# First pair's expert rows half gathered and half built, and one more weight buffer, in a two-layer mixture-of-experts encoder

## The chip, the cores and the metric

The kernel runs on one core of a Trainium2 chip. A core has TensorE (PE), which multiplies and transposes, VectorE (DVE), ScalarE (ACT), GpSimd (POOL) and SyncE (SP), which here issues nearly all weight transfers. Sixteen DMA engines bring data from device memory. The metric is the time of one execution on the device in microseconds (us).

## The reference

Two layers are computed on 512 tokens of width 1024. Each layer has a mixer (three kinds of attention) and then an expert-choice feed-forward part. Cut to what matters here, the second part is:

```python
def expert_choice_ffn(h, w_router, w_gate, w_up, w_down):
    affinity = jax.nn.softmax(h @ w_router, axis=-1)           # 512 tokens, 16 experts
    gate, idx = lax.top_k(jnp.swapaxes(affinity, 1, 2), 64)    # each expert takes 64 tokens
    xe = h[idx]                                                # rows of the chosen tokens
    a, u = xe @ w_gate[e], xe @ w_up[e]                        # 1024 -> 1408
    y = (jax.nn.silu(a) * u) @ w_down[e]                       # 1408 -> 1024
    return scatter_add(y * gate)                               # back to the tokens
```

`h` is the RMS-normalised `x`: each row is scaled by its own factor (`rstds`) and each feature by a gain (`gf`). All of it is in float32.

## The kernel before, in words

The 16 experts are taken as 8 pairs. An expert takes 64 tokens, so a pair fills 128 rows. Of each pair, `xe` holds the chosen rows feature-major, as 8 blocks `xe[:, k]` of 128 features by 128 rows.

**Weights.** For each pair the loop at L1206 loads 24 weight tiles of 1408 KB with `load` (L152): eight of `w_gate` (k = 0 to 7), eight of `w_up`, eight of `w_down`. In this text weight tile n of a layer is the n-th load, so that tiles 0 to 7 are the first pair's `w_gate`, 8 to 15 its `w_up`, 16 to 23 its `w_down`. The room of a tile comes from `extra` (L1088): `SEQ` (L35) gives the first 15 rooms in order (eleven rooms `x0` to `x10`, the three rooms `s0` to `s2` of another pool, and once the room `hx`), and after that 14 rooms (all but `hx`) come round in the same order. A load is issued from SP's queue in program order, and it waits there until the tile that last had the room has been used by TensorE. So load 15 waits for tile 0, load 16 for tile 1, and so on; from load 27 on it is always the tile 14 loads before. The first 15 loads are issued while the mixer and the router are still running.

**Rows of the first pair.** `places(0)` (L1116) makes a 0/1 matrix `at` scaled with `rstds`, in the room `xy`. `fill` (L1128) makes one block of `xe` as a product of `x` with `at` (4 products, 8 PE instructions), and VectorE multiplies by `gf` on the way out. `EARLY` (L57) says after which k which blocks are filled: block 0 ahead of tile 0, blocks 1 and 2 after it, and then one after each of the tiles 1 to 5.

**Rows of the other pairs.** `marks(p)` (L1140) compares the ranks with `iota` on VectorE (`oh`), multiplies on TensorE for each row's token number, scale and gate, and transposes `oh`; VectorE copies the results out. `fetch_rows(p)` (L1159) then lets GpSimd gather the 128 rows of 4 KB from `xrow_d` in device memory into `xy`, and ScalarE scales them (L1163). `turn_rows` (L1166) transposes four blocks (L1170), and VectorE multiplies them by `gf` (L1171). `marks(p + 1)` and the gather stand after k = 6 of pair p's `w_gate`; the transposes stand, in the program, after the pair's `w_up`. For pair 0 `marks(0)` is wanted only for the gates and the scatter, and stands after k = 2 of `w_up`.

**Order.** The framework orders each engine's instructions by a plan of its own. `keep_in_program_order` ties an instruction behind the one that was written ahead of it for the same engine. The weight products (L1215, L1252), the loads, the `fill` calls inside the loop and the comparison in `marks` are tied; the products and transposes in `marks` and the transposes of `turn_rows` are not, and may be taken earlier than they are written.

Of the kernel before, what the change touches and what calls it, by code (L numbers as in the profile page):

```python
# [22 lines left out]
P = 128  # L23
S = 512
# [7 lines left out]
CAP = 64  # L32
SLOT = 3072
RING = 3
SEQ = [0, 1, 4, 's0', 2, 3, 's2', 5, 6, 7, 9, 8, 'hx', 10, 's1']  # L35
PAD = 168
AFTER = [[2, 3, 5, 8], [1, 5, 7, 10], [2, 3, 6, 9]]
H_ON = 'vvvvavaa'
# [15 lines left out]
PLAN = [(0, 1), (1, 1), (2, 2), (3, 2), (4, 2), (0, 0), (1, 2), (5, 2)]  # L54
PART_ON = 'vvav'
START = [[6, 0, 2, 6, 4], [2, 0, 0, 4, 2]]
EARLY = [[(0, 1)], [(1, 1), (2, 1)], [(3, 1)], [(4, 1)], [(5, 1)], [(6, 1)], [(7, 1)], [], []]  # L57
END_ON = 'avavav'
MARK_AT = 6
VALUES_AT = 9  # L60
FIRST_MARKS = 2
SCATTER_AT = (2, 4)
HALVED = 8
EASE = 5
# [66 lines left out]
def body(ctx, tc, x_in, pos, w_in, w_uq, w_ukv, w_out, w_gate, w_up, w_down, gatt, gfin, params, consts, band, sel, out):  # L131
# [8 lines left out]
    def nm(s):  # L140
        uid[0] += 1
        return f"{s}_{uid[0]}"
# [711 lines left out]
    for l in range(L):  # L854
# [221 lines left out]
        with tc.tile_pool(name=f"fx{l}", bufs=1, reuse_waits="tile") as fx, tc.tile_pool(name=f"fw{l}", bufs=2, side="right", reuse_waits="tile") as fw:  # L1076
# [5 lines left out]
            def xslot(i):  # L1082
                return fx.tile([P, 2 * FF], F32, tag=f"x{i}", name=nm("xslot"))
# [3 lines left out]
            def extra():  # L1087

                n = hold["n"]
                hold["n"] += 1  # L1090
                again = [q for q in SEQ if q != "hx"]
                which = SEQ[n] if n < len(SEQ) else again[(n - len(SEQ)) % len(again)]
                if isinstance(which, int):
                    return first_x.pop(which) if which in first_x else xslot(which)
                return wide() if which == "hx" else slot(which)[:, : 2 * FF]
# [19 lines left out]

            def places(p):  # L1116

                at_ = fw.tile([P, D], F32, tag="xy", bufs=1, name=nm("at"))[:, :S].rearrange("p (t s) -> p t s", t=NT)
                for t in (0, 2):
                    chosen(at_, p, t, t + 2)  # L1120
                for t in range(NT):
                    if t < 2:
                        nc.scalar.activation(at_[:, t], at_[:, t], AF.Copy, scale=rstds[:, t : t + 1])
                    elif t % 2 == 0:
                        q = at_[:, t : t + 2]
                        nc.vector.tensor_tensor(q, q, rstds[:, t : t + 2].unsqueeze(2).to_broadcast([P, 2, P]), op=ALU.mult)
                return at_

            def fill(at_, xe, k0, n, pin=False):

                b = bank()
                for k in range(n):
                    c = (k0 + k) * P
                    for t in range(NT):
                        made = nc.tensor.matmul(b[:, k * P : (k + 1) * P], x[:, t, c : c + P], at_[:, t], start=(t == 0), stop=(t == NT - 1))
                        if pin:
                            tc.keep_in_program_order(made)
                nc.vector.tensor_tensor(xe[:, k0 : k0 + n, :], b[:, : n * P].rearrange("p (k s) -> p k s", k=n), gf[:, k0 : k0 + n].unsqueeze(2).to_broadcast([P, n, P]), op=ALU.mult)

            def marks(p):  # L1140

                oh = fw.tile([P, S], F32R, tag="oh", bufs=2, name=nm("oh"))
                o3 = oh.rearrange("p (t s) -> p t s", t=NT)
                tc.keep_in_program_order(chosen(o3, p, 0, NT))
                b, g = bank(), bank()
                for t in range(NT):
                    nc.tensor.matmul(g[:, 0:4], o3[:, t].bitcast(F32), info[:, t, p, :], start=(t == 0), stop=(t == NT - 1))
                for t in range(NT):
                    nc.tensor.transpose(b[:, t * P : (t + 1) * P], o3[:, t].bitcast(F32), ident)
                for i in range(2):  # L1150
                    nc.vector.tensor_copy(gates[64 * i : 64 * i + 64, p : p + 1], g[64 * i : 64 * i + 64, i : i + 1])
                if p > 0:
                    nc.vector.tensor_copy(token[:, p : p + 1], g[:, 2:3])
                    nc.vector.tensor_copy(scales[:, p : p + 1], g[:, 3:4])
                nc.vector.tensor_copy(oh, b)  # L1155
                return oh


            def fetch_rows(p):  # L1159

                v = fw.tile([P, D], F32, tag="xy", bufs=1, name=nm("rows"))
                nc.gpsimd.indirect_dma_start(v, None, xrow_d[l][:, :], bass.IndirectOffsetOnAxis(token[:, p : p + 1], 0))  # L1162
                nc.scalar.activation(v, v, AF.Copy, scale=scales[:, p : p + 1])  # L1163
                return v

            def turn_rows(v, xe, k0):  # L1166

                b = bank()
                for k in range(4):
                    nc.tensor.transpose(b[:, k * P : (k + 1) * P], v[:, (k0 + k) * P : (k0 + k + 1) * P], ident)  # L1170
                nc.vector.tensor_tensor(xe[:, k0 : k0 + 4, :], b.rearrange("p (k s) -> p k s", k=4), gf[:, k0 : k0 + 4].unsqueeze(2).to_broadcast([P, 4, P]), op=ALU.mult)  # L1171

            def gathered():
# [32 lines left out]
            for p in range(8):  # L1206
                acc = []
                for w in (w_gate, w_up):
                    bs = [bank() for _ in cuts]
                    acc.append(bs)  # L1210
                    for k in range(KD):
                        ws = load(w[l, p, k])
                        for b, (q0, qn) in zip(bs, cuts):
                            for i in range(2):
                                tc.keep_in_program_order(nc.tensor.matmul(b[64 * i : 64 * i + 64, : qn * NJ], xe[:, k, 64 * i : 64 * i + 64], ws[i][:, q0 * NJ : (q0 + qn) * NJ], start=(k == 0), stop=(k == KD - 1)))  # L1215
                        if w is w_gate and p == 0:
                            for f in EARLY[k + 1]:
                                fill(xg, xe, *f, pin=True)
                        if w is w_gate and k in SCATTER_AT and pending is not None:
                            scatter(*pending, 2 * SCATTER_AT.index(k))  # L1220
                        if w is w_up and k == FIRST_MARKS and p == 0:
                            ohs[0] = marks(0)
                        if w is w_gate and k == MARK_AT and p < 7:
                            ohs[p + 1] = marks(p + 1)
                            rows = fetch_rows(p + 1)
                hx = wide()
                hh, hT = hx[:, :FF].rearrange("p (j q) -> p j q", j=NJ), hx[:, FF:].rearrange("p (j s) -> p j s", j=NJ)
                for g, u, (q0, qn) in zip(acc[0], acc[1], cuts):
                    hv = hh[:, :, q0 : q0 + qn].rearrange("p j q -> p q j")
                    nc.scalar.activation(hv, g[:, : qn * NJ].rearrange("p (q j) -> p q j", j=NJ), AF.Silu)  # L1230
                    nc.vector.tensor_tensor(hv, u[:, : qn * NJ].rearrange("p (q j) -> p q j", j=NJ), hv, op=ALU.mult)  # L1231
                if p < 7:
                    nxt = gathered()
                    for k0 in (0, 4):
                        turn_rows(rows, nxt, k0)
                for j0, n in ((0, 4), (4, 4), (8, 3)):
                    b = bank()
                    for q in range(n):
                        nc.tensor.transpose(b[:, q * P : (q + 1) * P], hh[:, j0 + q, :], ident)
                    nc.vector.tensor_copy(hT[:, j0 : j0 + n, :], b[:, : n * P].rearrange("p (q s) -> p q s", q=n))  # L1240
                bs = [bank(), bank()]
                ahead = [(t, h) for t in range(NT - 1) for h in range(2)] if p == 7 else []
                whole = {}
                for lo in range(0, NJ * D, FF):
                    hi = lo + FF
                    ws = load(w_down[l, p, lo // FF])
                    e = lo
                    while e < hi:
                        j, h = e // D, e % D // 512
                        z = min(hi, (e // 512 + 1) * 512)  # L1250
                        for i in range(2):
                            tc.keep_in_program_order(nc.tensor.matmul(bs[h][64 * i : 64 * i + 64, e % 512 : e % 512 + z - e], hT[:, j, 64 * i : 64 * i + 64], ws[i][:, e - lo : z - lo], start=(j == 0), stop=(j == NJ - 1)))  # L1252
                        e = z
                    if ahead and lo > 0:
                        take_x(*ahead.pop(0))
                ys = results(p, bs)
                if p < 7:
                    pending = ohs.pop(p), ys
                    xe = nxt
# [133 lines left out]
```

## Time and profile before

| | |
|---|---|
| median of 3 runs | 1949.41 us (1947.63 to 1950.34) |
| the profiled execution: time, span | 1949.72 us, 1947.6 us |
| mean granted TensorE clock | 0.967 of full speed |
| busy share of the span: PE, DVE, ACT, POOL | 90%, 36%, 22%, 10% |
| moved by DMA | 646.71 MB, mean 332 GB/s |

The span runs from the first to the last instruction; the time is 2.1 us longer. The clock has two levels here: 1.00 in the rows is 2.4 GHz, 0.50 is 1.2 GHz. A row of a timeline gives start, duration, engine, line, operation, what it writes and reads, how many instructions were merged, and in brackets how long the engine had been idle and what ended it.

### The profile page before, as it was taken

The numbers are of one execution on the slowest core, as the hardware profiler recorded it, in microseconds if no ns is written. First come the engines' busy times: TensorE is split into PE (matmuls) and PEld (weight loads), VectorE is DVE, ScalarE is ACT, GpSimd is POOL, SyncE is SP. The second block draws the span as 40 slices with busy tenths as digits, with TensorE's granted clock in tenths as the row PEclk, the third lists the DMA queues.
The fourth block names the chain that finished last, engine by engine and source line by source line (L and its number), as shares of the span: only waits on it lengthen the run. The fifth ranks groups of instructions, "written<-read, shape, count | busy, mean of one in ns | idle before, by whom it ended". The sixth has DMA issues, their size and how long they took to land.

```text
span 1947.6 us, 22276 instructions
## 1 busy us (share of the span) xinstructions
PE 1747.3 (90%) x8894; PEld 914.8 (47%) x8894; DVE 709.2 (36%) x1483; ACT 426.2 (22%) x881; POOL 203.2 (10%) x230
## 2 busy tenths in 40 slices
PE   7999999898998988888899999998898998888887
PEld 6786665443333333333377856753333333333323
DVE  6877856121121111211168688551112112111112
ACT  4337951000100100000043489311100000001001
POOL 1314421000000000000013253100000000000000
PEclk8999998999999999999999999999999999999999
DMA  6765748899999999999938736689999999999996
GB/s 222 209 178 85 169 142 310 321 418 424 424 425 424 424 425 424 424 423 425 406 116 261 164 74 133 220 332 363 425 424 425 424 424 424 425 424 424 425 424 247
DMA packets 102471, 646.71 MB, mean 332 GB/s; under 512 B 11008, under 2 KB 28160, under 8 KB 53216
## 3 DMA queue, kind: packets, MB, share of 16 engines
q1 hardware_dynamic: 88336, 606.34, 77.7%
q0 software_dynamic: 11968, 35.02, 7.6%
q10 hardware_dynamic: 2064, 3.93, 0.6%
q8 instruction: 70, 1.15, 0.2%
q14 instruction: 33, 0.27, 0.0%
HBM read 616.55 MB, written 27.39 MB: 331 GB/s over the span
## 4 chain that ended last, share of the span: by engine, by line
DMA 43%; PE 38%; DVE 9%; issue 5%; ACT 3%; POOL 1%; SPq 0%; DVEq 0%; ACTq 0%; POOLq 0%
DMA xslot<-in_w_up_dram 13%; DMA xslot<-in_w_down_dram 10%; PE ps L1215 9%; DMA xslot<-in_w_gate_dram 8%; PE ps L732 7%; PE ps L1252 6%; DMA slot<-in_w_gate_dram 6%; PE ps L833 4%; DMA rows<-xrow_d,slots 4%; PE ps L741 2%; PE ps L650 2%; PE ps L633 1%; DVE sm L582 1%; DMA slot<-in_w_down_dram 1%; PE ps L493 1%
## 5 line engine op out<-in xcount | busy, mean ns | idle before, releaser
L1215 PE MATMUL ps<-xslot,xe 128*64 128x506 f32 (+1 forms) x2400 | 515.9, 575 | 29.1 <-DMA xslot<-in_w_up_dram 16.6
L1215 PEld LDWEIGHTS ps<-xslot,xe 128*64 128x64 f32 x2400 | 166.8, 140 | 351.7 <-issue 286.6
L1252 PE MATMUL ps<-xslot,hx 128*64 128x512 f32 (+3 forms) x1392 | 248.8, 506 | 22.5 <-DMA xslot<-in_w_down_dram 18.7
L1231 DVE TENSOR_TENSOR hx<-ps,hx 128x506 f32<-128x506 f32 (+1 forms) x48 | 43.0, 959 | 475.4 <-PE ps L1215 475.4
L1252 PEld LDWEIGHTS ps<-xslot,hx 128*64 128x64 f32 x1392 | 94.1, 137 | 165.0 <-issue 123.4
L1182 ACT ACTIVATE hx<-ps,gates 128x512 fp32r<-128x512 f32 x32 | 20.2, 683 | 675.9 <-PE ps L1252 675.9
L732 PE MATMUL ps<-xh,w 128*128 128x512 f32 (+1 forms) x448 | 147.6, 414 | 11.5 <-ACT xh L346 11.5
L1183 DVE SCALAR_TENSOR_TENSOR hx<-ps,gates,hx 128x512 fp32r<-128x512 f32 x32 | 22.6, 747 | 345.1 <-ACT hx L1182 345.1
L1215 PE MATMUL ps<-slot,xe 128*64 128x506 f32 (+1 forms) x648 | 140.0, 566 | 7.3 <-DMA slot<-in_w_gate_dram 5.7
L1193 DVE TENSOR_TENSOR x<-ps,x 128x512 f32<-128x512 f32 x112 | 69.6, 684 | 160.2 <-PE ps L1191 160.2
L589 ACT ACTIVATE P<-ps,sm 128x512 f32<-128x512 f32 x168 | 116.4, 702 | 32.1 <-DVE sm L582 30.9
L1162 POOL DMA_INDIRECT rows<-xrow_d,slots x14 | 13.8, 984 | 987.5 <-DVE oh L1155 914.6
L1163 ACT ACTIVATE rows<-rows,slots 128x1024 f32<-128x1024 f32 x14 | 16.1, 1147 | 444.9 <-DMA rows<-xrow_d,slots 444.9
L732 PEld LDWEIGHTS ps<-xh,w 128*128 128x128 f32 (+1 forms) x448 | 87.0, 195 | 35.7 <-ACT xh L346 12.5
L1215 PEld LDWEIGHTS ps<-slot,xe 128*64 128x64 f32 x648 | 45.1, 138 | 91.3 <-issue 74.7
L732 PE MATMUL ps<-xl,w 128*128 128x512 f32 (+1 forms) x224 | 85.7, 393 | 0.0
L1170 PE MATMUL ps<-ident,rows 128*128 128x128 f32 x112 | 27.0, 421 | 64.8 <-ACT rows L1163 64.8
L582 DVE TENSOR_REDUCE sm<-ps 128x1 f32<-128x512 f32 x120 | 78.9, 681 | 5.5 <-PE ps L567 4.9
L633 PE MATMUL ps<-ident,P 128*128 128x128 f32 x512 | 77.8, 275 | 1.2 <-ACT P L589 1.2
L1252 PE MATMUL ps<-slot,hx 128*64 128x512 f32 (+3 forms) x400 | 71.6, 497 | 6.3 <-DMA slot<-in_w_down_dram 4.8
L641 ACT COPY pt<-ps 128x512 f32<-128x512 f32 x118 | 68.8, 604 | 25.8 <-PE ps L633 25.5
L633 PEld LDWEIGHTS ps<-ident,P 128*128 128x128 f32 x512 | 62.5, 141 | 24.4 <-ACT P L589 7.0
(280 smaller groups left out, 2186.1 us busy)
## 6 DMA issues: line engine op xcount, KB each, us to landing
xslot<-in_w_gate_dram SPq DMA_DIRECT2D x100, 1408.0 KB, 26.4
xslot<-in_w_up_dram SPq DMA_DIRECT2D x100, 1408.0 KB, 27.0
xslot<-in_w_down_dram SPq DMA_DIRECT2D x100, 1408.0 KB, 27.0
slot<-in_w_gate_dram SPq DMA_DIRECT2D x28, 1408.0 KB, 27.0
slot<-in_w_down_dram SPq DMA_DIRECT2D x28, 1408.0 KB, 27.0
slot<-in_w_up_dram SPq DMA_DIRECT2D x26, 1408.0 KB, 27.5
slot<-in_w_in_dram SPq DMA_DIRECT2D x8, 1536.0 KB, 7.2
st<-bst_d POOLq DMA_DIRECT2D x40, 256.0 KB, 4.2
```

Source lines behind the costliest of these rows:

```text
L582: nc.vector.tensor_reduce(mn, ps, axis=AX.X, op=ALU.min)
L589: nc.scalar.activation(e, ps, AF.Exp, bias=mn, scale=-1.0, accum_out=lcol)
L633: nc.tensor.transpose(b[:, kc * P : (kc + 1) * P], e[:, kc * P : (kc + 1) * P], ident)
L641: nc.scalar.copy(dv, bv)
L650: nc.tensor.matmul(o[64 * i : 64 * i + 64], heads[2 * m + i][4][:, kc, :], pts[i][:, kc, :], start=(kc == 0), stop=(kc == NT - 1))
L732: nc.tensor.matmul(b[:m], w[:, passes[j][0], k, :m], passes[j][1](k), start=(n == 0), stop=(n == 3 * KD - 1))
L741: nc.tensor.matmul(acc[t][:, :m], xs, w[:, c, kk, :], start=(k == 0 and j == 0), stop=(k == KD - 1 and j == 2))
L833: nc.tensor.matmul(blocks[t][1 + h], o, w[h], start=(i == 0), stop=(i == 3 * KD - 1))
L1193: nc.vector.tensor_tensor(xv, b, xv, op=ALU.add)
L1215: tc.keep_in_program_order(nc.tensor.matmul(b[64 * i : 64 * i + 64, : qn * NJ], xe[:, k, 64 * i : 64 * i + 64], ws[i][:, q0 * NJ : (q0 + q ...
L1231: nc.vector.tensor_tensor(hv, u[:, : qn * NJ].rearrange("p (q j) -> p q j", j=NJ), hv, op=ALU.mult)
L1252: tc.keep_in_program_order(nc.tensor.matmul(bs[h][64 * i : 64 * i + 64, e % 512 : e % 512 + z - e], hT[:, j, 64 * i : 64 * i + 64], ws[i][ ...
```

## The change

The first pair's blocks 4 to 7 are no longer made by `fill` but gathered and transposed as for the other pairs: `marks(0)` and `fetch_rows(0)` move to just behind tile 0 and the fills of blocks 1 and 2 (`FIRST_MARKS = 0`), and the transposes with the product by `gf` stand behind tile 3 (`HALF_AT = 3`). `marks(0)` now also copies out token numbers and scales. The gathered rows of every pair go into `x0`, the room of weight tile 0, which weights then have only once; `xy` is gone, and `at` takes one of the two rooms of `oh`. A room `x11` joins, so the first 16 loads have rooms of their own, and 14 rooms come round as before. The transposes of `turn_rows` are tied to their place, in all pairs.

```diff
-SEQ = [0, 1, 4, 's0', 2, 3, 's2', 5, 6, 7, 9, 8, 'hx', 10, 's1']
+SEQ = [0, 1, 4, 's0', 2, 3, 's2', 5, 6, 7, 9, 8, 'hx', 10, 11, 's1']
-EARLY = [[(0, 1)], [(1, 1), (2, 1)], [(3, 1)], [(4, 1)], [(5, 1)], [(6, 1)], [(7, 1)], [], []]
+EARLY = [[(0, 1)], [(1, 1), (2, 1)], [(3, 1)], [], []]
+HALF_AT = 3
-FIRST_MARKS = 2
+FIRST_MARKS = 0
...
-                again = [q for q in SEQ if q != "hx"]
+                again = [q for q in SEQ if q not in (0, "hx")]
...
-                at_ = fw.tile([P, D], F32, tag="xy", bufs=1, name=nm("at"))[:, :S].rearrange("p (t s) -> p t s", t=NT)
+                at_ = fw.tile([P, S], F32R, tag="oh", bufs=2, name=nm("at")).bitcast(F32).rearrange("p (t s) -> p t s", t=NT)
...
-                if p > 0:
-                    nc.vector.tensor_copy(token[:, p : p + 1], g[:, 2:3])
-                    nc.vector.tensor_copy(scales[:, p : p + 1], g[:, 3:4])
+                nc.vector.tensor_copy(token[:, p : p + 1], g[:, 2:3])
+                nc.vector.tensor_copy(scales[:, p : p + 1], g[:, 3:4])
...
-                v = fw.tile([P, D], F32, tag="xy", bufs=1, name=nm("rows"))
+                v = xslot(0)[:, :D]
...
-                    nc.tensor.transpose(b[:, k * P : (k + 1) * P], v[:, (k0 + k) * P : (k0 + k + 1) * P], ident)
+                    tc.keep_in_program_order(nc.tensor.transpose(b[:, k * P : (k + 1) * P], v[:, (k0 + k) * P : (k0 + k + 1) * P], ident))
...
-                            for f in EARLY[k + 1]:
+                            for f in EARLY[k + 1] if k + 1 < len(EARLY) else ():
                                 fill(xg, xe, *f, pin=True)
+                            if k == FIRST_MARKS:
+                                ohs[0] = marks(0)
+                                rows = fetch_rows(0)
+                            if k == HALF_AT:
+                                turn_rows(rows, xe, 4)
...
-                        if w is w_up and k == FIRST_MARKS and p == 0:
-                            ohs[0] = marks(0)
```

## Rows read from the trace of the kernel before

**Rows 1.** The page's 40 slices of the span: GB/s moved by DMA.

```profile
GB/s 222 209 178 85 169 142 310 321 418 424 424 425 424 424 425 424 424 423 425 406 116 261 164 74 133 220 332 363 425 424 425 424 424 424 425 424 424 425 424 247
```

**Rows 2.** Windows of both feed-forward parts: busy time by engine, clock, DMA share, GB/s.

```profile
core 0: us, PE busy (x) PEld busy (x) DVE busy (x) ACT busy (x) POOL busy (x), PEclk, DMA share, GB/s
...
336.00:341.00 5.00, 4.62 (x23) 2.68 (x23) 0.48 (x2) 0.20 (x1) 0.00 (x0) 0.85 0.03 14
341.00:376.00 35.00, 30.14 (x176) 15.29 (x175) 5.40 (x17) 0.33 (x1) 1.23 (x1) 0.99 0.94 362
376.00:381.00 5.00, 4.13 (x14) 2.34 (x16) 0.00 (x0) 2.10 (x2) 0.00 (x0) 0.50 0.41 173
...
401.00:551.00 150.00, 137.08 (x706) 56.85 (x704) 27.51 (x49) 9.78 (x12) 1.90 (x2) 0.95 1.01 425
...
1345.00:1600.00 255.00, 234.33 (x1234) 97.14 (x1231) 47.88 (x82) 18.55 (x23) 2.83 (x3) 0.97 1.01 423
```

**Rows 3.** The page's DMA issues: KB each, median us from issue to landing.

```profile
xslot<-in_w_gate_dram SPq DMA_DIRECT2D x100, 1408.0 KB, 26.4
...
slot<-in_w_out_dram POOLq DMA_DIRECT2D x4, 512.0 KB, 6.4
```

**Rows 4.** Timeline of TensorE in the first pair, layer 0, and layer 1's tile 0.

```profile
338.22 2.58 PE L1215 MATMUL ps<-xslot,xe 128*64 128x506 f32 x12 [0.38 <-DVE xe L1138]
340.73 2.05 PE L1135 MATMUL ps<-at,x 128*128 128x128 f32 x16
342.71 2.58 PE L1215 MATMUL ps<-xslot,xe 128*64 128x506 f32 x12
...
346.32 2.58 PE L1215 MATMUL ps<-xslot,xe 128*64 128x506 f32 x12
...
363.24 1.06 PE L1147 MATMUL ps<-slots,oh 128*128 128x4 f32 x8
364.15 0.63 PE L1149 MATMUL ps<-ident,oh 128*128 128x128 f32 x4
364.72 4.95 PE L1215 MATMUL ps<-xslot,xe 128*64 128x506 f32 x24
...
376.87 1.97 PE L1170 MATMUL ps<-ident,rows 128*128 128x128 f32 x8 [5.73 <-ACT rows L1163]
378.77 8.82 PE L1215 MATMUL ps<-xslot,xe 128*64 128x506 f32 x36
...
1295.89 2.58 PE L1215 MATMUL ps<-xslot,xe 128*64 128x506 f32 x12 [0.38 <-DVE xe L1138]
```

**Rows 5.** Timeline of SP's queue: loads 14, 15, 16, 24 of layer 0; 24 of layer 1.

```profile
327.36 0.53 SPq L154 DMA_DIRECT2D slot<-in_w_up_dram  x1
340.84 0.33 SPq L154 DMA_DIRECT2D xslot<-in_w_up_dram  x1
345.34 3.93 SPq L154 DMA_DIRECT2D xslot<-in_w_down_dram  x2
...
382.91 9.78 SPq L154 DMA_DIRECT2D xslot<-in_w_gate_dram  x4
...
1339.53 5.05 SPq L154 DMA_DIRECT2D xslot<-in_w_gate_dram  x3
```

**Rows 6.** Timeline of all engines, layer 0: the first `marks` and its gather.

```profile
342.82 0.29 DVE L1138 TENSOR_TENSOR xe<-ps,pgf 128x128 f32<-128x128 f32 x1 [0.60 <-PE ps L1135]
...
361.04 0.68 DVE L1109 TENSOR_TENSOR oh<-iota,code 128x512 fp32r<-128x512 f32 x1
...
365.84 1.23 POOL L1162 DMA_INDIRECT rows<-xrow_d,slots  x1 [37.23 <-issue]
...
375.67 1.15 ACT L1163 ACTIVATE rows<-rows,slots 128x1024 f32<-128x1024 f32 x1 [39.47 <-DMA rows<-xrow_d,slots]
```

**Rows 7.** The tile `rows`, all 14 gathers: time from issue to landing.

```profile
DMA to landing us min/median/max: 9.2/9.7/10.4
```

**Rows 8.** Groups from 336 to 1945 us: busy, mean ns of one, idle before.

```profile
L1170 PE MATMUL ps<-ident,rows 128*128 128x128 f32 x112 | 27.0, 421 | 64.8 <-ACT rows L1163 64.8
...
L1239 PE MATMUL ps<-ident,hx 128*128 128x128 f32 x176 | 22.7, 278 | 21.5 <-DVE hx L1231 21.5
...
L1171 DVE TENSOR_TENSOR xe<-ps,pgf 128x512 f32<-128x512 f32 x28 | 17.9, 682 | 0.0
```

## The prediction

> **What bounds the kernel now.** I read the slices first. From slice 8 to slice 18, counted from 0, and from 28 to the last but one, DMA moves 418 to 425 GB/s without a dip [rows 1]. The windows say the same of the long stretches of both feed-forward parts: DMA share 1.01 at 423 to 425 GB/s, while TensorE is busy for 137.08 of 150 us and waits for the rest [rows 2]. There the stream of weights sets the time. A tile of 1408 KB [rows 3] is 1,441,792 bytes, at 424.5 GB/s 3.40 us; TensorE needs only 4.95 / 2 = 2.48 us for one [rows 4]. So whatever lies on TensorE in pairs 1 to 7 has cover, and a layer's end is fixed by the moment from which the stream no longer stops. The sum is made for that moment.
>
> It lies in the first pair. Between 336 and 341 us DMA moves 14 GB/s, between 376 and 381 us 173 GB/s, between them 362 GB/s [rows 2]. The queue says why. Load 14 is issued at 327.36, and load 15 must wait for tile 0, until 340.84; load 16 waits for tile 1 (345.34) [rows 5]. Loads 16 to 23 then follow TensorE, which takes 3.61 us for a tile with its fill (342.71 to 346.32) [rows 4], longer than a load. Then TensorE stops: the transposes of pair 1's rows, which are not tied, were taken in front of tile 9 and wait 5.73 us for the gather, and afterwards run at half clock [rows 2, 4]. Tile 9 is not released until 382.91, and that is when load 24 is issued [rows 5]; from there on the stream does not stop. In layer 1 load 24 is at 1339.53 [rows 5].
>
> **The change, part by part (layer 0).**
>
> *marks(0) behind tile 0.* The comparison is tied behind VectorE's product for block 2, which ends at 342.82 + 0.29 = 343.11; it takes 0.68 [rows 6], so `oh` is there at 343.8. Tile 1 is tied behind the transposes of `marks`, which with its products take 1.48 us (363.24 to 364.72) [rows 4]. Tile 1 starts at 345.3 instead of 342.71: 2.6 us later, an idle 1.0 and the 1.5 of work. It is released 2.63 us after its start, as before (342.71 to 345.34): load 16 goes out at 347.9. Tile 2 follows after 3.6 (block 3 is still filled), at 348.9, tile 3 at 351.4, done at 353.9.
>
> *The gather.* GpSimd issued 2.60 us after the products of `marks` had begun (363.24 to 365.84) [rows 4, 6]: 346.4 here. The room `x0` is no obstacle, since tile 0 is done at 340.8. The landing has no row under the conditions that the change makes. From above: all 14 gathers took 9.2 to 10.4 us [rows 7], each beside a full stream. From below: GpSimd's plain transfers of 512 KB, the gather's size, took 6.4 [rows 3]. Here DMA is idle at the issue, and one load (16) goes out 1.5 us later and shares the engines with it; I take 8.4, the middle, so the rows are there at 354.8. ScalarE has nothing else and takes 1.15 [rows 6]: 356.0.
>
> By the Trainium skill ("DMA: Bandwidth & Descriptors", section "Anatomy of one DMA — SWDGE (gpsimd) path") a transfer issued by GpSimd takes some 2.0 us plus its bytes at 436 GB/s, which would be an estimate of 3.2 us here; the rows stand against it with 9.2 us at the least [rows 7]. By the page the gather would be no wait at all, and the sum would end at the bound given below for an early landing.
>
> *Half of the rows turned behind tile 3.* These transposes are tied, so TensorE waits for them: from 353.9 to 356.0 idle, 0.63 for four (as the four of `marks`) [rows 4], 0.68 for VectorE's product [rows 8] and 0.1 for the hand-overs. Tile 4 starts at 357.4 (about 353.5 before, three times 3.61 behind tile 1), and is released at 360.0; then load 19 goes out. Behind the waiting transpose stands all of TensorE's work, and behind that only the loads. The other queues (VectorE, ScalarE, GpSimd) have nothing due in between.
>
> *Fills of blocks 4 to 7 gone.* Tiles 4, 5 and 6 now follow each other after 2.5 instead of 3.61. They are released at 360.0, 362.5 and 365.0, tile 7 (with `marks(1)` ahead of it) at 369.0, tiles 8 and 9 at 371.5 and 374.0.
>
> *marks(0) and the early transposes gone from in front of tile 9.* That stretch now holds 369.60 to 378.77 us on the clock of before. After the change it holds nothing: the transposes are tied behind tile 15, where TensorE waits 21.5 / 16 = 1.34 us for VectorE anyway [rows 8], and eight of them take 1.2 to 1.3 us.
>
> *The sixteenth buffer.* Load 15 needs no release; it follows load 14 at about 328 and fills the hole from 336 on. Load 16 still waits for tile 1 and every later load for the same tile as before. The extra 3.40 us of stream are therefore not a saving by themselves: DMA then idles up to load 16, longer than before. Its worth is that load 15 no longer stands between tile 0 and load 16. `x11` lies where the router's work tiles were, as does `x10`, whose load goes out just ahead of load 14; even if it were late by 10 us, it would land ahead of load 16.
>
> *The sum.* Loads 16, 17 and 18 and the gather (524,288 bytes, 1.24 us) are 11.4 us of stream from 347.9, that is to 359.3; load 19 is issued at 360.0, so the release of tile 4 decides, by 0.7 us. From load 19 on every release is ahead of the stream (362.5 against 363.4, 365.0 against 366.8, 369.0 against 370.2, then 2 us and more). Up to load 24 there are 5 loads, 17.0 us, and pair 1's gather, which used to run in a stretch with slack: 1.24 us. Load 24 stands at 378.2 instead of 382.91: 4.7 us gained. Layer 1 begins tile 0 at 1295.89, 957.67 after layer 0, so load 24 would stand at 1335.9 instead of 1339.53: 3.7 us. Together 8.4 us. From there both kernels have the same loads; later pairs lose 64.8 us of TensorE waiting at L1170 [rows 8], which gives nothing because DMA is full. Against the profiled execution's 1949.72 us this is **1941.3 us**; that execution is 0.3 us above the median of the runs.
>
> *Bounds of the one unknown price.* Landing after 6.4: the rows are 2.0 us earlier, but the stream's own 359.3 then decides, and each layer gains 0.7 more: 1939.9. Landing after 10.4: tile 4 is 2.0 us later in each layer: 1945.3.
>
> **The rivals.**
>
> *Half clock after the new wait (chance 0.18).* TensorE stands for 2.1 us, with the hand-over to VectorE nearly 3. Before, a wait of 5.73 us was followed by clock 0.50 [rows 2, 4]; waits of 1.34 us were followed by transposes of 278 ns [rows 8], full speed. Mine lies between, nearer the shorter. If the clock falls, four transposes cost some 0.4 more (eight took 1.97 us at half clock, four 0.63 at full) and the next tiles 1.4 more (8.82 us for three instead of 7.4) [rows 4]. Load 19 is 1.8 us later in each layer: 1944.9, and with a landing after 10.4 us 1948.9, which is no measurable change.
>
> On this the Trainium skill ("TensorE: Matmul & The Clock Gate", section "HAM oscillation — how this bites in real kernels") says that waiting for a transfer between two tiles throttles the clock, so that the next tile starts cold. The half clock after L1170 agrees [rows 2]; no row here shows what a wait of 2 to 3 us does.
>
> *The gather comes late (slower; chance 0.14).* The same wait is now in front of everything, where before it was met after tile 8. The place is tile 4, the price 1 us of end for each us that tile 4 is late, in each layer. The gain is gone when load 19 slips by 4.7 and 3.7 us: a landing 12.6 us after the issue on average, or 10.8 if the clock falls too. For slower by 0.2% (3.9 us) it takes 14.6, or 12.8. No row reaches that [rows 7], and the queue in front of this gather is emptier than in any of them.
>
> *Nothing moves (chance 0.08).* If loads 16 to 18 or the rooms of the first round were held by something else than TensorE, the line from load 19 would not hold, and the end would stay near 1949. The queue's times match the tiles' ends too closely for that [rows 4, 5].
>
> *TensorE sets the pace after all (chance 0.03).* If the 64.8 us at L1170 [rows 8] had no cover, tying the transposes would give up to 65 us more: some 1880. The full stream speaks against it [rows 1, 2].
>
> **How the numbers follow.** About 0.2% (3.9 us) is what a measurement of this kernel can tell from no change. The forecast, 1939.9 to 1945.3, has 0.57. Half clock has 0.18, and half of that ends within 0.2%. Of the late gather's 0.14, 0.10 is slower by more than 0.2%, the rest within. So faster is 0.57 + 0.09 + 0.03 = 0.69, within 0.2% is 0.09 + 0.04 + 0.08 = 0.21, slower 0.10. The range reaches from 1938.5, a little below the lower bound, since the sum's hand-overs are good to some tenths in each of two layers, to 1950.0: it takes in half clock to its far end and the case that nothing moves, and leaves out the gather that makes it slower and the 65 us, 0.13 in all.
>
> **What the profile after would show.** Load 16 at about 9.7 us after tile 0 starts, load 19 at 21.8, load 24 at 40.0 (44.69 before); DMA idle from about 339 to 349 and then no second hole; one wait of some 2 us at L1170 ahead of tile 4 and none in later pairs; no clock of 0.50 there; GB/s unchanged at 424 after it. It would prove me wrong if the wait ahead of tile 4 were over 5 us, if the clock fell, if a second hole in the stream appeared between loads 19 and 28, or if TensorE instead of DMA ended the layers.

## The result, and the profile after

The changed kernel takes 1936.34 us in the median of four runs (1935.47 to 1937.56), the kernel before 1949.88 us in four runs beside them: ratio 0.9937, interval 0.9925 to 0.9949. That is faster, by 13.5 us, where 8.4 were forecast; the time lies 2.2 us below the range. The profiled execution took 1935.57 us with a span of 1933.8.

The page's slices of the kernel after answer to [rows 1]: slice 7 moves 352 GB/s instead of 321, slice 8 is full, and in layer 1 slice 27 moves 418 instead of 363.

```profile
GB/s 223 205 186 85 163 151 337 352 423 425 425 424 424 424 425 425 425 423 425 403 116 262 158 82 126 227 318 418 424 425 424 424 425 424 424 424 425 425 425 252
```

The windows of layer 0 after the change, with the columns of [rows 2]:

```profile
339.00:347.50 8.50, 7.43 (x51) 4.67 (x51) 2.63 (x9) 0.00 (x0) 1.09 (x1) 1.00 0.25 78
347.50:381.00 33.50, 32.72 (x174) 12.53 (x172) 2.44 (x7) 6.21 (x6) 0.97 (x1) 1.00 1.00 411
...
400.00:550.00 150.00, 140.04 (x744) 56.77 (x742) 28.83 (x50) 11.11 (x14) 1.87 (x2) 1.00 1.01 424
```

TensorE in the first pair, layer 0, answers to [rows 4]:

```profile
335.82 2.58 PE L1215 MATMUL ps<-xslot,xe 128*64 128x506 f32 x12 [0.38 <-DVE xe L1139]
...
341.46 1.03 PE L1148 MATMUL ps<-slots,oh 128*128 128x4 f32 x8 [1.07 <-DVE oh L1110]
...
351.39 0.65 PE L1170 MATMUL ps<-ident,xslot 128*128 128x128 f32 x4
352.83 2.58 PE L1215 MATMUL ps<-xslot,xe 128*64 128x506 f32 x12 [0.78 <-DVE xe L1171]
...
382.97 1.09 PE L1170 MATMUL ps<-ident,xslot 128*128 128x128 f32 x8
```

The transposes of the fetched rows (351.39) start with no wait in brackets; between tile 0 and tile 15 TensorE's only waits are 1.07 us for the comparison and 0.78 us for VectorE's product. Those of pair 1 (382.97) now stand behind tile 15 and wait for nothing, where before they waited 5.73 us in front of tile 9. The gather and ScalarE's scaling, and SP's queue, answer to [rows 6] and [rows 5]:

```profile
343.87 1.09 POOL L1162 DMA_INDIRECT xslot<-xrow_d,slots  x1 [9.52 <-PE ps L1150]
...
348.54 1.15 ACT L1163 ACTIVATE xslot<-xslot,slots 128x1024 f32<-128x1024 f32 x1 [14.09 <-DMA xslot<-xrow_d,slots]
```
```profile
327.14 0.43 SPq L155 DMA_DIRECT2D slot<-in_w_up_dram  x1
345.54 3.93 SPq L155 DMA_DIRECT2D xslot<-in_w_down_dram  x2
351.50 0.33 SPq L155 DMA_DIRECT2D slot<-in_w_down_dram  x1
355.45 4.32 SPq L155 DMA_DIRECT2D xslot<-in_w_down_dram  x2
...
368.90 12.14 SPq L155 DMA_DIRECT2D xslot<-in_w_gate_dram  x5
```

Load 15 goes out at 327.14, load 16 at 345.54 (9.72 us after tile 0), load 19 at 355.45 (19.63 after tile 0), load 24 at 368.90 (33.08 after tile 0, where before it was 44.69). From the gather's issue to ScalarE's start are 4.67 us. Over all 16 gathers of the kernel after, an answer to [rows 7], only the first pair's are that quick:

```profile
DMA to landing us min/median/max: 4.5/9.4/10.5
```

**Where the 13.5 us came from.** I cut the execution at four rows: the start of each layer's tile 0, and the end of its last product with `w_down`. Of the kernel before and of the one after, the last such product in each layer:

```profile
966.91 4.90 PE L1252 MATMUL ps<-xslot,hx 128*64 128x256 f32 x28
...
1923.87 5.05 PE L1252 MATMUL ps<-xslot,hx 128*64 128x256 f32 x28
```
```profile
958.77 4.90 PE L1255 MATMUL ps<-xslot,hx 128*64 128x256 f32 x28
...
1909.99 5.01 PE L1255 MATMUL ps<-xslot,hx 128*64 128x256 f32 x28
```

With tile 0 at 338.22 and 1295.89 before [rows 4], and at 335.82 and 1286.34 after, and with the further profiles of both kernels told of below (four profiles of before, three of after):

| us | before, each profile | after, each profile | gain of the means | forecast |
|---|---|---|---|---|
| start to tile 0, layer 0 | 338.22, 337.07, 337.41, 336.37 | 335.82, 335.23, 337.05 | 1.2 | 0 |
| feed-forward products, layer 0 | 633.59, 633.43, 633.56, 632.83 | 627.85, 628.25, 629.37 | 4.9 | 4.7 |
| from there to tile 0, layer 1 | 324.08, 324.17, 325.36, 325.47 | 322.67, 322.55, 323.60 | 1.8 | 0 |
| feed-forward products, layer 1 | 633.03, 633.74, 633.94, 634.12 | 628.66, 627.81, 627.65 | 5.7 | 3.7 |
| from there to the end | 18.68, 18.59, 18.63, 18.61 | 18.80, 18.76, 18.83 | -0.2 | 0 |

Both feed-forward parts together gain 10.5 us. The other 2.9 lie in stretches that the change does not touch.

### The profile page after: what moved, and what is told of

Same layout as the page of the kernel before. It is cut to its first block, busy times and chain, and to the rows that moved or that the text cites. A ratio compares the mean times of both kernels' runs of the same rounds, so it can differ in the third digit from the quotient of the medians.

```text
span 1933.8 us, 22166 instructions
## 1 busy us (share of the span) xinstructions
PE 1729.4 (89%) x8838; PEld 888.7 (46%) x8838; DVE 709.3 (37%) x1481; ACT 429.0 (22%) x883; POOL 205.6 (11%) x232
## 4 chain that ended last, share of the span: by engine, by line
DMA 51%; PE 35%; DVE 9%; ACT 3%; issue 1%; POOL 1%; SPq 0%; DVEq 0%; ACTq 0%; POOLq 0%
DMA xslot<-in_w_up_dram 12%; DMA xslot<-in_w_gate_dram 11%; DMA xslot<-in_w_down_dram 10%; PE ps L1215 7%; PE ps L733 6%; DMA slot<-in_w_up_dram 6%; DMA slot<-in_w_gate_dram 6%; DMA slot<-in_w_down_dram 6%; PE ps L834 4%; PE ps L1255 4%; PE ps L742 2%; PE ps L651 2%; PE ps L634 2%; DVE sm L583 1%; PE ps L494 1%
## 5 line engine op out<-in xcount | busy, mean ns | idle before, releaser
L1215 PEld LDWEIGHTS ps<-xslot,xe 128*64 128x64 f32 x2400 | 162.0, 137 | 410.7 <-issue 260.2
L1162 POOL DMA_INDIRECT xslot<-xrow_d,slots x16 | 15.3, 959 | 961.2 <-DVE oh L1155 942.2
L1163 ACT ACTIVATE xslot<-xslot,slots 128x1024 f32<-128x1024 f32 x16 | 18.4, 1148 | 442.9 <-DMA xslot<-xrow_d,slots 442.9
L333 DVE TENSOR_TENSOR w<-slot,w 128x1024 fp32r<-128x1024 f32 (+4 forms) x46 | 53.8, 1171 | 30.2 <-ACT w L332 27.2
```

The costliest lines, as they stand in the source:

```text
L333: nc.vector.tensor_tensor(w[:, 1, :, o : o + m], src, w[:, 0, :, o : o + m].bitcast(F32), op=ALU.subtract)
```

## The experiments

My theory after the result: the end of a layer is fixed by the moment from which the weight stream no longer stops, and the wait in front of tile 9 is the stop that the change removes. The rivals: the rework of the first pair's rows pays by itself, or the sixteenth buffer does. The expectations say what each gives. In the results "feed-forward" means the two stretches of the table, layer 0 and layer 1.

**One part alone: the tie.** The kernel before, with nothing but the tied transposes.

```diff
-                    nc.tensor.transpose(b[:, k * P : (k + 1) * P], v[:, (k0 + k) * P : (k0 + k + 1) * P], ident)
+                    tc.keep_in_program_order(nc.tensor.transpose(b[:, k * P : (k + 1) * P], v[:, (k0 + k) * P : (k0 + k + 1) * P], ident))
```

> The kernel before, with only the transposes of turn_rows tied to their place. Theory A (the stream is worth what its last hole costs, and the hole at tile 9 is made by TensorE waiting for pair 1's gather): the wait in front of tile 9 goes, tile 8 is released at 369.7 and tile 9 at 373.7 on the clock of before, so load 23 follows load 22 without a gap, load 24 stands at about 375.4 instead of 382.91, and each layer gains 6.4 to 7.5 us: about 1935.5 us, as much as the whole change. Theory B (the half gathered rows, the shorter fills and the sixteenth buffer make the gain): tying alone gives at most a few us, 1945 or more.

Measured: 1934.57 us (1934.02 to 1935.80), ratio 0.9929, interval 0.9916 to 0.9943; feed-forward 626.51 and 627.06, so 6.8 and 6.7 us gained against the means of before. TensorE, POOL, ScalarE and SP's queue around tile 9, layer 0:

```profile
368.84 7.31 PE L1215 MATMUL ps<-xslot,xe 128*64 128x506 f32 x36
...
385.54 1.09 PE L1170 MATMUL ps<-ident,rows 128*128 128x128 f32 x8
```
```profile
363.62 1.23 POOL L1162 DMA_INDIRECT rows<-xrow_d,slots  x1 [35.62 <-issue]
```
```profile
373.35 1.15 ACT L1163 ACTIVATE rows<-rows,slots 128x1024 f32<-128x1024 f32 x1 [38.74 <-DMA rows<-xrow_d,slots]
```
```profile
371.47 9.78 SPq L154 DMA_DIRECT2D xslot<-in_w_gate_dram  x4
```

The gather is as slow as before (9.7 us from issue to ScalarE), but nothing waits for it: tiles 9 to 11 take 7.31 us, at full clock, instead of 8.82 behind 7.70 us of waiting and turning [rows 4]. Load 24 goes out at 371.47, which is 35.48 us after this kernel's tile 0 (335.99) instead of 44.69. The tie by itself gives as much as the whole change.

**The rework without the tie in later pairs.** The change, with only the first pair's transposes tied.

```diff
-                    tc.keep_in_program_order(nc.tensor.transpose(...))
+                    made = nc.tensor.transpose(...)
+                    if xe is first:
+                        tc.keep_in_program_order(made)
```

> The changed kernel, with the transposes tied for the first pair alone; those of pairs 1 to 7 are free again and will be taken early, as in the kernel before. Theory A: TensorE waits 2 to 4 us for pair 1's gather behind tile 8, but tile 9 is then done at about 37 us after tile 0 starts, and the stream brings load 24 only at 38.2, so nothing is lost: 1936 to 1938 us, and TensorE waits some 4 us in every later pair without effect. Rival (tying the transposes in all pairs is what gained): 1944 us or more.

Measured: 1937.11 us (1936.11 to 1938.53), ratio 0.9940, interval 0.9926 to 0.9953; feed-forward 627.20 and 627.73. The early transposes are back, in both layers, and TensorE waits in front of them in this kernel's timeline:

```profile
369.66 1.09 PE L1170 MATMUL ps<-ident,xslot 128*128 128x128 f32 x8 [2.50 <-ACT xslot L1163]
370.69 7.31 PE L1218 MATMUL ps<-xslot,xe 128*64 128x506 f32 x36
...
1320.92 1.50 PE L1170 MATMUL ps<-ident,xslot 128*128 128x128 f32 x8 [1.92 <-ACT xslot L1163]
1322.35 8.54 PE L1218 MATMUL ps<-xslot,xe 128*64 128x506 f32 x36
```

and over both layers in its groups, an answer to [rows 8]:

```profile
L1170 PE MATMUL ps<-ident,xslot 128*128 128x128 f32 x120 | 26.4, 390 | 58.1 <-ACT xslot L1163 58.1
```

58.1 us of waiting cost nothing that the feed-forward times show: with the rework TensorE is ahead of the stream when it meets the wait (load 24 still goes out 36.82 us after tile 0 in layer 0 and 37.88 in layer 1). The tie and the rework are two ways to remove the same hole; their gains do not add up.

**The change without the sixteenth buffer.** `x11` is taken out, `x0` is again among the 14 rooms that come round, and the fetched rows get the old room `xy`.

```diff
-SEQ = [0, 1, 4, 's0', 2, 3, 's2', 5, 6, 7, 9, 8, 'hx', 10, 11, 's1']
+SEQ = [0, 1, 4, 's0', 2, 3, 's2', 5, 6, 7, 9, 8, 'hx', 10, 's1']
...
-                again = [q for q in SEQ if q not in (0, "hx")]
+                again = [q for q in SEQ if q != "hx"]
...
-                v = xslot(0)[:, :D]
+                v = fw.tile([P, D], F32, tag="xy", bufs=1, name=nm("rows"))
```

> The changed kernel without the sixteenth buffer: 15 rooms as before, x0 among the 14 that come round, and the gathered rows in a room of their own (xy) as before. Theory A: load 15 waits for tile 0 and runs in the time in which DMA is idle anyway, load 16 still waits for tile 1: no change against the changed kernel, 1936 us within 1.5. Rival (one buffer more is one tile of 3.40 us ahead in each layer): 6.8 us slower than the changed kernel, 1943 us.

Measured: 1936.97 us (1936.23 to 1939.00), ratio 0.9944, interval 0.9931 to 0.9958; feed-forward 627.40 and 629.06. In its queue load 15 again waits for tile 0 (335.92), and load 16 goes out 9.71 us after it, as in the whole change:

```profile
338.54 0.33 SPq L155 DMA_DIRECT2D xslot<-in_w_up_dram  x1
345.63 3.93 SPq L155 DMA_DIRECT2D xslot<-in_w_down_dram  x2
```

The buffer is worth nothing that this measurement can tell.

**The gather made late.** The first pair's gather is issued twice into the same room, the second behind the first; the rows come out the same.

```diff
-                nc.gpsimd.indirect_dma_start(v, None, xrow_d[l][:, :], ...)
+                for _ in range(2 if p == 0 else 1):
+                    nc.gpsimd.indirect_dma_start(v, None, xrow_d[l][:, :], ...)
```

> The changed kernel with the first pair's gather issued twice, the second one after the landing of the first, into the same room; nothing else differs. Theory A (the prediction's step: from the moment at which the rows are later than tile 3, each us is a us of the end, in each layer; the gain was larger because the rows came after 4.6 us, not 8.4): the rows are ready 10 to 13 us after the first issue, TensorE waits 4 to 6 us in front of tile 4, perhaps at half clock afterwards, and the end is 4 to 6 us later in each layer: 1944 to 1949 us, most or all of the gain gone. Rival (the landing is not what was mis-sized; the stream has slack there): 1936 to 1939 us.

Measured: 1956.86 us (1953.32 to 1960.23), ratio 1.0047, interval 1.0035 to 1.0059: slower than before. What the first pair's two gathers of layer 0 took from issue to landing, the second one's issue, the loads around it, a window of the time that it took, and TensorE in front of tile 4:

```profile
DMA to landing us min/median/max: 4.6/7.1/9.7
```
```profile
348.51 0.97 POOL L1163 DMA_INDIRECT xslot<-xrow_d,slots  x1 [3.73 <-DMA xslot<-xrow_d,slots]
```
```profile
345.37 3.93 SPq L155 DMA_DIRECT2D xslot<-in_w_down_dram  x2
351.33 0.33 SPq L155 DMA_DIRECT2D slot<-in_w_down_dram  x1
```
```profile
350.00:358.30 8.30, 1.29 (x8) 0.28 (x4) 0.00 (x0) 0.00 (x0) 0.00 (x0) 0.75 0.99 383
```
```profile
359.52 1.11 PE L1171 MATMUL ps<-ident,xslot 128*128 128x128 f32 x4 [8.23 <-ACT xslot L1164]
361.42 4.05 PE L1216 MATMUL ps<-xslot,xe 128*64 128x506 f32 x12 [0.78 <-DVE xe L1172]
```

The same transfer takes 4.6 us where DMA is idle at its issue and 9.7 us beside loads 16 to 18, which with it move 383 GB/s. Load 19 goes out 29.87 us after tile 0 instead of 19.63, 10.2 us later (10.0 in layer 1); feed-forward is 636.68 and 636.64, 8.2 and 8.6 us longer than with the change. So the late-gather rival is a real mechanism, at nearly its price (0.80 and 0.86 us for each us). The rows were there 14.6 us after the first issue; the rival, which counts with a half clock behind the wait, had the gain gone at 10.8 and 2 us of end for each us beyond: 7.6 us slower. Measured are 9.2 (1956.86 against 1947.69), with 1.2 us of extra transfer in each layer. The 1944 to 1949 us that I had expected were too low: beside the three loads the second gather took twice as long as the first, and the clock fell behind the wait.

**The marks earlier.** The first pair's comparison goes ahead of block 0, its products ahead of tile 0; the gather stays behind tile 0, which frees its room.

```diff
+            oh = compared(0)
             for f in EARLY[0]:
-                fill(xg, xe, *f)
-            ohs = {}
+                fill(xg, xe, *f, pin=True)
+            ohs = {0: marks(0, oh)}
...
                             if k == FIRST_MARKS:
-                                ohs[0] = marks(0)
                                 rows = fetch_rows(0)
```

Run on two chips, the second time beside the changed kernel itself.

> The changed kernel with the comparison of marks(0) made ahead of block 0's product on VectorE and its products and transposes ahead of tile 0 on TensorE; the gather still follows tile 0. Theory A (the release of tile 1 sets the stream from load 16 on): tile 0 starts 1.1 us later, tile 1 is released 1.4 us earlier, and the end moves by the same in each layer: 2.5 to 3 us faster than the changed kernel, 1933.5 us. Rival (the stream is set by tile 4 or something behind it): no change, 1936 us.

> The best version so far once more, beside the changed kernel on one chip. Theory A (load 16 is 1.5 us earlier and the clock does not fall near tile 1, since TensorE no longer idles there): 3 to 5 us faster than the changed kernel. Rival (the first comparison was scatter): within 1.5 us.

> The changed kernel, unchanged, for comparison on the same chip as the other runs of this call: 1935 to 1937.5 us; load 16 at 9.72 us after tile 0 in both layers unless the clock falls near tile 1, as it did in layer 1 of the first profile (11.35).

Measured: 1931.94 us (1930.46 to 1934.19), ratio 0.9918, interval 0.9904 to 0.9931; on the second chip 1930.66 us (1929.76 to 1933.52), ratio 0.9914, interval 0.9902 to 0.9927. There the changed kernel took 1935.76 us (1934.39 to 1938.32), ratio 0.9943, interval 0.9930 to 0.9956. So this version is 5.1 us faster than the change, and the fastest of all; I had expected 2.5 to 3 us at first, then 3 to 5. Its feed-forward takes 624.40 and 624.53, then 625.16 and 624.71. Tile 0 starts at 336.89, and its timeline shows no 1.07 us wait between tiles 0 and 1, and load 16 released 7.12 us after tile 0 instead of 9.72:

```profile
335.44 1.02 PE L1153 MATMUL ps<-slots,oh 128*128 128x4 f32 x8
336.32 0.63 PE L1155 MATMUL ps<-ident,oh 128*128 128x128 f32 x4
336.89 2.58 PE L1221 MATMUL ps<-xslot,xe 128*64 128x506 f32 x12
339.40 2.05 PE L1136 MATMUL ps<-at,x 128*128 128x128 f32 x16
341.38 2.58 PE L1221 MATMUL ps<-xslot,xe 128*64 128x506 f32 x12
```
```profile
344.01 3.93 SPq L155 DMA_DIRECT2D xslot<-in_w_down_dram  x2
```

**Four more profiles, for the stretches that the change does not touch.**

> The kernel before, unchanged, once more, to see when tile 0 of layer 0 starts; up to there the order of instructions is the same in every kernel here. It started at 338.22 us in the first profile of before and at 335.8 to 336.5 in the changed kernel and three relatives. Theory A (the 2.4 us are scatter of the clock in the router, not an effect of the change): tile 0 starts at 335.8 to 336.5 this time, or with a second value that no edit explains. Rival (something in the change speeds up the part ahead of the feed-forward): 338.2 again.

> The kernel before, unchanged, one look. It asks whether the earlier start of layer 0's first weight product (335.82 us after the change, 338.22 before) belongs to the kernels or scatters from execution to execution. Theory A (it belongs to them): tile 0 starts at 337.0 to 338.3, and TensorE's low clock in the router lasts some 10 us again. Theory B (it scatters): at least one of two looks starts below 336.5.

> The kernel before once more, with the same two expectations: 337.0 to 338.3 by theory A, a start below 336.5 in one of the two looks by theory B.

> The changed kernel, one look, beside the two of the kernel before. Theory A: tile 0 of layer 0 starts at 335.2 to 336.0. Theory B: as late as 337 can occur. It also asks whether the half clock in layer 1 after the 1.07 us wait at the marks comes back: it did in one of two profiles; if it depends on when the wait falls, either may be seen, and layer 1 from tile 0 to the end takes 647.5 us with it and 646.6 without.

Measured: spans 1947.0, 1948.9 and 1947.4 of the kernel before, 1936.5 of the one after; the rest is in the table above. The theory that the start scatters holds as it was written: one profile of before starts tile 0 at 336.37 and one of after only at 337.05, so the two overlap. In the mean, before still starts 1.2 us later. The windows of the router from 330 to 335 us show what goes with it. First the kernel before, its first profile, then a later one, then the kernel after, its first profile and a later one (clock third from the right):

```profile
330.00:335.00 5.00, 4.55 (x16) 1.89 (x16) 2.73 (x14) 0.00 (x0) 0.00 (x0) 0.50 1.00 421
```
```profile
330.00:335.00 5.00, 3.88 (x19) 1.33 (x17) 3.47 (x14) 0.69 (x2) 0.00 (x0) 0.87 0.98 354
```
```profile
330.00:335.00 5.00, 3.96 (x23) 1.86 (x22) 3.35 (x13) 0.69 (x2) 0.92 (x3) 0.95 0.99 387
```
```profile
330.00:335.00 5.00, 4.55 (x17) 1.88 (x16) 2.81 (x11) 0.60 (x2) 0.92 (x3) 0.50 1.01 428
```

In either kernel the clock is back at 2.4 GHz early or late in the router, and tile 0 follows 1 to 2 us earlier or later. Three of four profiles of before had it late and one of three of after; whether the change shifts the odds, or chance did, these profiles cannot say.

## Why the prediction was right in direction and wrong in size

**What set the time: right.** After the change DMA again moves 424 GB/s through the long stretch, and the moment from which the stream no longer stops decides. The experiments follow it: the earlier or later loads 16 to 24 can go out (the marks ahead, the change, the late gather), the shorter or longer are the feed-forward parts, while TensorE's waits behind that moment (58.1 us with the tie in the first pair only) leave no mark.

The weights can be counted. 60 us after the start of tile 0, layer 0, the stream of before had delivered 27.8 tiles: the first 15, and 316 GB/s for 60 us less one gather. After the change it is 29.5: the first 16 less the 1.34 MB that still came in the first 6 us, and 365 GB/s for 60 us less two gathers.

```profile
338.22:398.22 60.00, 53.10 (x280) 24.11 (x280) 7.98 (x20) 5.05 (x5) 1.23 (x1) 0.94 0.81 316
```
```profile
335.82:341.82 6.00, 4.92 (x32) 3.02 (x32) 1.18 (x3) 0.00 (x0) 0.00 (x0) 1.00 0.53 223
335.82:395.82 60.00, 57.42 (x321) 25.24 (x323) 10.65 (x24) 6.21 (x6) 2.06 (x2) 1.00 0.89 365
```

Counted so in both layers and all profiles, it is 27.7 to 28.1 tiles before, 29.1 to 29.6 after, 29.9 and 30.0 with the tie alone, 30.4 with the marks earlier and 26.8 with the late gather. At 3.40 us a tile these four are in the mean 5.5, 7.3, 8.8 and -3.4 us ahead of before; their feed-forward parts are 5.3, 6.7, 8.8 and -3.1 us shorter.

**Marks behind tile 0, and load 16: right.** Forecast 9.7 us after tile 0, measured 9.72; the idle time of 1.0 us was 1.07.

**The gather's landing: wrong, by half.** I took 8.4 us, between 9.2 to 10.4 [rows 7] and 6.4 [rows 3]; measured are 4.3 to 4.7 us in three profiles. The 6.4 was no lower bound: a median over GpSimd's plain transfers says nothing on what else moves beside them. I had seen that DMA is idle at the issue, and still kept to rows taken beside a stream. By the Trainium skill ("DMA: Bandwidth & Descriptors", section "Anatomy of one DMA — SWDGE (gpsimd) path") the estimate was 3.2 us; the idle-queue landing of 4.6 us is nearer to it than to my rows, and the 9.7 us beside loads 16 to 18 is not what its formula gives. So the wait of 2.1 us in front of tile 4 does not exist, and load 19 goes out at 19.63 instead of 21.8: the case that I had as the bound of an early landing.

**The stream from there on: also wrong, on both sides.** I let it run at full rate from load 16 on. From 345.54 to 383 us it moved 404 GB/s, 20 below full, which is 1.8 us of that stretch, and it starts slowly: of 345.5 to 347.0 the window shows 191.

```profile
345.50:347.00 1.50, 1.50 (x12) 1.10 (x14) 0.29 (x1) 0.00 (x0) 0.00 (x0) 1.00 0.77 191
```
```profile
345.54:383.00 37.46, 36.68 (x193) 14.34 (x193) 4.11 (x10) 6.21 (x6) 0.97 (x1) 1.00 0.99 404
```

Loads 16 to 19 go out 2.4 to 4.0 us apart (345.54 and 3.6 us later, 351.50, 355.45), about the 3.40 that one takes, so that the start of each is little covered by the one before; that this is the reason was not tried by itself. But the stream of before was as slow when it started again behind load 24: 356 GB/s in the first 10 us (349 to 357 over both layers of its four profiles), 1.6 us less than full.

```profile
382.91:392.91 10.00, 10.00 (x52) 3.52 (x50) 0.00 (x0) 2.62 (x3) 0.00 (x0) 1.00 0.90 356
```

The forecast set its 40.0, a place in the stream, against 44.69, the issue of load 24 in the kernel before, and left this out. (Load 24 itself was issued at 33.08, ahead of the stream; I had forecast its release for 35.8.) In layer 0 the early landing (0.7 us more gain), the slow stream after the change (1.8 less) and the slow restart before it (1.6 more) nearly cancel: 4.9 us gained, 4.7 forecast. That this size came out so close is luck.

**Layer 1: 5.7 instead of 3.7.** Load 24 of before stands at 43.64 us after tile 0 in the profile that I used, and at 45.59, 44.77 and 44.75 in the three others: 1.0 us of the miss of 2.0 is that one profile was the quickest. On the other side, the first profile after has half clock there: behind the 1.07 us wait at the marks, tile 1 takes 3.94 us instead of 2.58, and load 16 goes out 11.35 us after tile 0.

```profile
1291.98 1.03 PE L1148 MATMUL ps<-slots,oh 128*128 128x4 f32 x8 [1.07 <-DVE oh L1110]
1292.86 0.92 PE L1150 MATMUL ps<-ident,oh 128*128 128x128 f32 x4
1293.71 3.94 PE L1215 MATMUL ps<-xslot,xe 128*64 128x506 f32 x12
```

The two later profiles of the same kernel have the same wait without the fall, and 627.81 and 627.65 us instead of 628.66. So about 0.9 us; the half-clock rival was real, but at a place where I had put no chance on it. The kernel without `x11` shows it once more there in layer 1 (load 16 again 11.35 us after tile 0). This lengthens the time after the change, so it explains nothing of the miss; at least 1 us of it stays without a cause.

**The rest of the span: 2.9 us, forecast 0.** This is the step that failed by most. The sum left the start of tile 0 in layer 0 and the stretch between the two feed-forward parts as they were before, and so put at nothing whatever lies outside those parts. The 2.9 us are in the mixers and the router, whose code is the same. In part they go with the clock (above); their cause is not settled. Outside the feed-forward parts the four profiles of before take 679.8 to 681.4 us, the three of after 676.5 to 679.5, and the one with the tie alone 678.3, although its edit touches only the transposes of pairs 1 to 7. Of the 5 us by which the forecast fell short, 2.1 are in the feed-forward parts, nearly all in layer 1, and 2.9 here; without these 2.9 the time would have come out inside the range.

**Tying in later pairs, and the sixteenth buffer: right.** Each is worth nothing beside the rest (1937.11 and 1936.97 against 1936.34 us). But I counted the wait in front of tile 9 as gone by the whole rework and did not ask what the tie does by itself: either of the two removes it, and the smaller one gave as much.

## What to carry to other kernels

Where a stream of transfers sets the time, look for the last moment at which it stops, and ask for each part of a change alone whether it removes that stop: here one tied line did as much as a rework of five places. A transfer's price belongs to what moves beside it; take its duration from a row with the same load on the queues, or bound it well below the rows that have more. A forecast to a few us needs more than one profile of the kernel before: all its stages but the last differed by 0.8 to 1.9 us from profile to profile.

## What the runs showed of the hardware

The same gather of 512 KB takes 4.2 to 4.7 us when DMA is idle at its issue (eight profiles, both layers), 9.2 to 10.4 beside a full stream [rows 7], and 9.7 beside loads 16 to 18.

A stream of 1408 KB loads that starts again on idle engines is not at once at its full 424 GB/s: behind load 24 of the kernel before it moved 356 in the first 10 us.

Whether TensorE's clock falls behind a wait is not read from the length of the wait: 2.50 us in front of the transposes was followed by full clock (7.31 us for three tiles), 1.92 us at the same place in layer 1 by half clock (8.54), and 1.07 us at the marks, in layer 1, by half clock in one profile of the changed kernel out of three. The Trainium skill ("TensorE: Matmul & The Clock Gate", section "HAM oscillation — how this bites in real kernels") has the clock fall where TensorE waits for a transfer between two tiles; the 8.23 us wait in front of tile 4 agrees (the next tile took 4.05 us instead of 2.58); the 2.50 us wait shows that not every such wait does it.
